# A hybrid decoder step on one core: where attention's merge, key casts, square roots and the sample's steps stand, and a second copy of v

## The chip, the cores and the metric

The kernel runs on one core of a Trainium2 chip. The core has five engines with instruction streams of their own: TensorE (PE in the profile; its weight loads are PEld), VectorE (DVE), ScalarE (ACT), GpSimd (POOL) and SyncE (SP), which here mostly issues transfers. Sixteen DMA engines carry the transfers. The metric is device time in microseconds (us) of one execution; the figure for a kernel is the median of its runs.

## The reference

One layer of a decoder is computed for a prompt of 2048 tokens and for a sample of 8 requests with 4 tokens each. All sizes: model width 1024, four recurrence heads of 128, eight attention heads of 64, hidden width 2816.

```python
a = rmsnorm(x, norm_attn_g)
qa, fa, ia, ga, qb, kb, vb = jnp.split(a @ w_in, pts, axis=-1)
s_new, o_a = gla_chunked(q_a, k_a, v_a, jnp.log(forget), hgrn_s0, chunk)
o_a = rmsnorm(o_a, hgrn_onorm_g) * jax.nn.silu(ga)
o_b = dilated_attn_prompt(q_b, k_b, v_b)      # the sample: against cached keys and values
h = x + jnp.concatenate([o_a, o_b], -1) @ w_o
...
h = h + (jax.nn.silu(c) * (hn @ w_up)) @ w_down
h = h + gate * (p_emb @ w_ple_proj)
```

The attention has three dilations, 1, 4 and 16, each over its own window. The parts of the dilations are combined by their maxima and sums (`combine_dilations`). The keys and values of the prompt, the recurrence's states and the sample's shifted caches are outputs too.

## The kernel before

**Stages.** `in_phase` runs twice, for 1024 and for 1056 tokens, and computes the seven projections. Each goes to a scratch tensor in DRAM: `qT_d` and `kT_d` with features on partitions, `v_d` by token, `ha_d` and `va_d` for the recurrence. During the first run, `down_weights` also prepares combinations of the down projection's weights, and in the second run most units of the recurrence (`hgrn_unit`) are computed. Then comes the attention stage (`attn_phase`), with the rest of the side work beside it, and then `trunk`: output projection (`out_block`), feed-forward block (`ffn_block`) and embedding block (`embed_block`), three blocks of tokens each.

**Attention by units and turns.** Four pairs of heads (p = 0 to 3) are worked off. Each has two passes (`di`): pass 0 takes queries and keys by residue modulo 4, pass 1 takes blocks of 128 neighbouring tokens. Both have four chunks (c) of 512 tokens. The masks hold the counts of the dilations, so that two passes serve for three. A pair has 40 units, so there are 160. The loop over x (here: a turn) gives each turn the scores of one unit (L814 and L815, with `kH` and `kL`, the rounded key and its remainder), then on VectorE the masked row minimum (L819) and on ScalarE the exponential (L820). Every second turn it transposes the probabilities of two older units (L827, copied out at L829) and multiplies those of two still older ones with v (L839). At pairs 0 to 2 all of pass 0 comes first; at pair 3 the passes alternate.

**What is hung on the turns.** A table `todo` holds functions by turn. `stage` loads q and k of the next chunk seven turns before `stack` splits them: `stack` rounds q on GpSimd (L152), takes the remainder (L704), casts k to `kH` on ScalarE (L707) and takes `kL` on GpSimd (L708). `values_chunk` loads v six turns before a chunk begins: in pass 0 by one transfer (L734), in pass 1 by four (L737), one for each residue, since the rows that go to one group of partitions are four tokens apart. When a chunk's pass 1 is summed, `merge` is hung on six later turns, +0, +2, +3, +7, +10 and +11: read the statistics of both passes back (L745), row minimum (L753) and weights, normalization (L757 to L760), transposition (L763) and the way of the coefficients through DRAM to all partitions (L766, L770, tile `cf`, two buffers), the products with the two partial outputs on GpSimd (L775), and their sum (L777), on VectorE for pairs 0 to 2 and on GpSimd for pair 3, which is stored to `mix_d`.

**Side work.** The generator `others` holds the recurrence's last unit (`hgrn_unit` with `apart=True`), the sample's attention (`attn_sample`) and the sample's recurrence (`hgrn_sample`). It advances by one step after each of the first 27 turns and then after every second turn, and what is left follows at the end. Its steps are traced with a higher priority.

**What sets the order.** In the attention stage PE's order is that of the program (`manual_schedule`). On all other engines, and on SP's queue, a planner decides from a simulated course of time when an instruction stands in its engine's stream; it may put an instruction ahead of others if it takes its inputs to be there. Each engine then works strictly in that order, so an instruction whose input is late holds all behind it. `keep_in_program_order` binds an instruction behind the one that the program issued before it on the same engine. `issue_after(recent[0].ins)` binds the loads for `down_weights` behind a named store on SP's queue.

**Roots.** The reciprocal root of a mean square is computed by `rsqrt_small` on VectorE: a shift and a subtraction on the integer form (L104, L105) and three rounds of three instructions (L107 to L109).

Of the kernel before, what the change touches and what calls it, by code (L numbers as in the profile page):

```python
# [16 lines left out]
ALU = mybir.AluOpType  # L17
# [31 lines left out]
def hymba_step_kernel(ctx: ExitStack, tc: tile.TileContext, I: dict, O: dict):  # L49
# [26 lines left out]
    ones = const.tile([128, 128], F32, name="ones")  # L76
    V.memset(ones, 1.0)

    mask = early.tile([128, 768], F32, name="mask")
    qT_s = early.tile([128, 4, NS], F32, name="qT_s")  # L80
    kT_s = early.tile([128, 4, NS], F32, name="kT_s")
# [3 lines left out]
    qT_d = dram.tile([128, 4, SEQ], F32, name="qT_d")  # L85
    kT_d = dram.tile([128, 4, SEQ], F32, name="kT_d")
    v_d = dram.tile([SEQ, 512], F32, name="v_d")
    va_d = dram.tile([SEQ, 512], F32, name="va_d")
    ha_d = [dram.tile([128, 4, NTOK], F32, name=f"ha{i}_d") for i in range(3)]
    mix_d = dram.tile([128, NK, NTOK], F32, name="mix_d")  # L90
# [5 lines left out]

    def f32(ap):
        return ap.bitcast(F32)

    def rsqrt_small(pool, v, shape):  # L100
        i = pool.tile(shape, I32, name="rs_i")
# [122 lines left out]
    def in_phase(bi, tiles, shared, wp, ev, sm, pmm, pms, plv, po):  # L224
# [102 lines left out]
        def token_group(g, kind, w):  # L327
            late = None

            for j in (0, 1, 8, 2, 3, 4, 5, 6, 7) if bi else range(8):  # L330
# [47 lines left out]
                if smp:  # L378
                    if kind in "kv":
                        for b in range(8):  # L380
                            SP.dma_start(O["s" + kind][b, SEQ - 4:SEQ], o[4 * b:4 * b + 4])
                else:
                    if kind == "k":
                        SP.dma_start(O["pk"][tok:tok + 128], o)
                    if kind == "v":
                        SP.dma_start(O["pv"][tok:tok + 128], o)
                        recent[:] = [SP.dma_start(v_d[tok:tok + 128], o)]
                    if kind == "i":
                        SP.dma_start(va_d[tok:tok + 128], o)
                yield  # L390
# [49 lines left out]
    def hgrn_unit(u, heads, S, ld, wk, sp, plv, po, pms, msk, diag, apart=False):  # L440
# [130 lines left out]
            yield  # L571
        v = sp.tile([128, 2, 4], F32, name="o_v")
        V.tensor_scalar(v, ssq, 1.0 / 128, EPS, op0=ALU.mult, op1=ALU.add)
        r = rsqrt_small(sp, v.rearrange("p h c -> p (h c)"), [128, 8])
        if apart:
            yield
        for i, h in enumerate(heads):
# [15 lines left out]
    def hgrn_sample(hp, pps):  # L593
# [76 lines left out]
        v = hp.tile([128, 1], F32, name="hsv")  # L670
        A.activation(o, ops, AF.Square, accum_out=v)
        V.tensor_scalar(v, v, 1.0 / 128, EPS, op0=ALU.mult, op1=ALU.add)
        r = rsqrt_small(hp, v, [128, 1])
        V.tensor_scalar(o, ops, r, None, op0=ALU.mult)
        yield
        pt = pps.tile([128, 4, 128], F32, name="s1")
# [8 lines left out]
    def attn_phase(spare, rest):  # L685
# [9 lines left out]
                out.append(t)  # L695
            return out

        def stack(c, q, k):
            cs = slice(512 * c, 512 * c + 512)
            js = slice(128 * c, 128 * c + 128)  # L700
            split = "p (i r) -> p r i"
            for hh in range(2):
                round_g(qS[:, hh, cs], q[:, hh])
                G.tensor_sub(qS[64:, hh, cs], q[64:, hh], f32(qS[64:, hh, cs]))  # L704
            for hh in range(2):
                t = k[:, hh].rearrange(split, r=4)
                A.copy(kH[:, hh, :, js], t)  # L707
                G.tensor_sub(kL[:, hh, :, js], t, f32(kH[:, hh, :, js]))  # L708

        first = stage(0, 0, [t[:, :1024].rearrange("p (h t) -> p h t", h=2) for t in spare])  # L710
# [18 lines left out]
        def values_chunk(p, di, c):  # L729

            raw = wk.tile([128, 4, 128], F32, name="v", bufs=6)
            cols = v_d[512 * c:512 * c + 512, 128 * p:128 * p + 128]
            if di == 0:
                SP.dma_start(raw, cols.rearrange("(i r) c -> i r c", r=4))  # L734
            else:
                for r in range(4):
                    SP.dma_start(raw[32 * r:32 * r + 32], cols.rearrange("(n i r) c -> r i n c", i=32, r=4)[r])  # L737
            vals[p, di, c] = raw

        stats_d = [dram.tile([SEQ, 4], F32, name=f"stat{p}_d") for p in range(4)]  # L740
        coef_d = [[dram.tile([16, 128], F32, name=f"coef{p}{c}_d") for c in range(4)] for p in range(4)]

        def merge(p, c, parts, both):

# [27 lines left out]
                             .to_broadcast([64, 1024]))  # L772
            yield
            for i in range(2):
                G.tensor_mul(parts[i], parts[i], cf[:, i])  # L775
            yield
            (G if p == 3 else V).tensor_add(parts[1], parts[1], parts[0])  # L777
            SP.dma_start(mix_d[:, 4 + p, 512 * c:512 * c + 512], parts[1])

        class Block:  # L780
# [82 lines left out]
        for p in range(4):  # L863
            for c in range(4):
                x = begin[p, 0, c]
                if p:

                    x = begin[p, 0, 0] - 10 + 4 * c
                    at(x - 7, lambda p=p, c=c: staged.append(stage(p, c)))
                    at(x, lambda p=p, c=c: stack(c, *staged.pop(0)))  # L870
                elif c:
                    at(x - 12, lambda c=c: staged.append(stage(0, c)))
                    at(x - 6, lambda c=c: stack(c, *staged.pop(0)))
                for di in range(2):
                    at(begin[p, di, c] - 6, lambda p=p, di=di, c=c: values_chunk(p, di, c))
# [4 lines left out]
        def sums(u, x):  # L880
# [5 lines left out]
            if bl.r == 3:  # L886
# [3 lines left out]
                if di == 0:  # L890
                    outs[c] = o
                    SP.dma_start(stats_d[p][512 * c:512 * c + 512].rearrange("(i r) c -> i r c", r=4),
                                 bl.st.rearrange("p n h c -> p n (h c)"))
                else:
                    merge_at([x + d for d in (0, 2, 3, 7, 10, 11)], p, c, (outs[c], o), bl.both)

        for x in range(n + 19):
            if x < n:
# [758 lines left out]
    with tc.manual_schedule(engines={mybir.EngineType.PE}):  # L1657
        for turn in itertools.count(1):
            if next(main) == "last":
                break  # L1660
            if turn % 2 == 0 or turn < 28:
                first(side, 1)
        first(side, 1000)
    step(main, 1000)
# [160 lines left out]
```

## Time and profile before

| | |
|---|---|
| median of 3 runs | 2998.84 us (2991.91 to 3001.22) |
| profiled execution | 2996.88 us |
| its span, first to last instruction | 2995.1 us |
| mean granted clock of TensorE | 0.987 |
| attention stage | about 825 to 1195 us of the span |
| trunk | from about 1193 us to the end |

The profile is one execution. Its groups, waits and windows give busy times and the idle time of an engine ahead of an instruction, with the engine or transfer that ended it ("<-"). A row of the order of time begins with its start and its length in us. TensorE's granted clock is a share of its full speed; at 0.5 a matmul takes twice as long.

### The profile page before, as it was taken

How to read it: one execution, taken by the hardware profiler on the slowest of the kernel's cores; microseconds unless marked ns; L12 is line 12 of the kernel's file. 1: busy time of each engine (PE TensorE's matmuls, PEld its weight loads, DVE VectorE, ACT ScalarE, POOL GpSimd, SP SyncE). 2: the span in 40 equal slices, each digit the busy share in tenths (PEclk: the TensorE clock that was granted, in tenths of full speed). 3: DMA queues.
4: the chain of work that ended last, by engine and by line, in shares of the span. 5: the costliest groups of instructions: out<-in, count | busy, mean ns of one | idle time of the engine just before them, and what ended most of it. 6: DMA issues, size and time to landing. Idle time of an engine off the chain costs nothing.

```text
span 2995.1 us, 52434 instructions
## 1 busy us (share of the span) xinstructions
PE 2899.1 (97%) x18895; PEld 2700.5 (90%) x18895; DVE 2163.4 (72%) x4717; ACT 1318.4 (44%) x2856; POOL 674.0 (23%) x792
## 2 busy tenths in 40 slices
PE   8999999999989898999999999999999999999998
PEld 8987789887777677999999999999999999999998
DVE  6656758657386467569987888766679777677777
ACT  5333423222276576335444444544444544444443
POOL 1443222212143563103443431000001000000000
PEclk9999999999999999999999999999999999999998
DMA  5898634324349996766766668777779777778773
GB/s 179 297 355 305 206 105 120 99 80 124 123 114 279 249 234 177 258 233 210 243 203 204 203 200 293 236 242 243 252 242 308 251 237 243 245 261 295 267 268 132
DMA packets 342036, 659.88 MB, mean 220 GB/s; under 512 B 62928, under 2 KB 134736, under 8 KB 339984
## 3 DMA queue, kind: packets, MB, share of 16 engines
q1 hardware_dynamic: 304928, 468.42, 49.0%
q0 software_dynamic: 33264, 121.13, 12.8%
q10 hardware_dynamic: 3584, 66.98, 6.2%
q8 instruction: 149, 2.44, 0.3%
q14 instruction: 111, 0.91, 0.1%
HBM read 509.46 MB, written 213.92 MB: 242 GB/s over the span
## 4 chain that ended last, share of the span: by engine, by line
PE 59%; issue 17%; DMA 10%; DVE 9%; POOL 2%; ACT 2%; SPq 1%; POOLq 0%; DVEq 0%; ACTq 0%
PE mm L146 13%; PE mm L148 13%; PE mm L147 13%; PE mm L348 2%; PE mm L349 2%; PE mm L350 2%; POOL w L1296 1%; DMA cf<-coef_d 1%; PE acc L839 1%; PE PT L827 1%; PE S L814 1%; DMA xr<-in_xT_dram 1%; PE lv L485 1%; DVE w L185 1%; DMA draw<-in_w_down_dram 1%
## 5 line engine op out<-in xcount | busy, mean ns | idle before, releaser
L147 PE MATMUL mm<-w 128*128 128x348 f32 (+3 forms) x3636 | 1166.1, 321 | 1.3 <-DVE w L1456 0.8
L146 PE MATMUL mm<-w 128*128 128x348 f32 (+3 forms) x3508 | 1108.7, 323 | 18.7 <-ACT s L1254 6.2
L148 PE MATMUL mm<-w 128*128 128x348 f32 (+3 forms) x3508 | 1117.3, 321 | 2.0 <-DVE w L185 2.0
L147 PEld LDWEIGHTS mm<-w 128*128 128x128 f32 x3636 | 684.1, 188 | 4.1 <-DVE w L1088 2.0
L146 PEld LDWEIGHTS mm<-w 128*128 128x128 f32 x3508 | 656.2, 188 | 26.6 <-ACT s L1254 8.7
L148 PEld LDWEIGHTS mm<-w 128*128 128x128 f32 x3508 | 659.0, 188 | 3.3 <-DVE w L185 2.6
L185 DVE TENSOR_TENSOR w<-raw,w 128x512 fp32r<-128x512 f32 x586 | 421.1, 723 | 176.2 <-ACT w L184 168.6
L184 ACT CAST w<-raw 128x512 fp32r<-128x512 f32 x586 | 360.9, 621 | 413.1 <-PE mm L148 288.8
L1296 POOL DMA_DIRECT2D w<-wd_d x231 | 124.3, 538 | 899.2 <-PE mm L148 793.4
L1312 DVE TENSOR_TENSOR h<-h,mm 128x348 f32<-128x348 f32 (+1 forms) x504 | 247.7, 507 | 44.8 <-PE mm L148 43.5
L820 ACT ACTIVATE P<-P,st 128x256 f32<-128x256 f32 (+3 forms) x256 | 134.0, 526 | 60.0 <-DVE st L819 56.4
L1254 ACT COPY s<-mm 128x348 f32<-128x348 f32 (+1 forms) x198 | 88.0, 445 | 152.2 <-PE mm L148 151.9
L819 DVE CUSTOM_DVE_ANT_0 P<-S,mask 128x256 f32<-128x256 f32 (+3 forms) x256 | 104.4, 448 | 62.0 <-PE S L815 40.2
L348 PE MATMUL mm<-wh,xh 128*128 128x512 f32 x352 | 140.8, 403 | 0.1
L349 PE MATMUL mm<-wl,xh 128*128 128x512 f32 x352 | 140.7, 401 | 0.2 <-DVE wl L271 0.2
L350 PE MATMUL mm<-wh,xl 128*128 128x512 f32 x352 | 140.3, 399 | 0.0
L146 PE MATMUL mm<-xh,wh 128*128 128x384 f32 (+2 forms) x384 | 124.6, 329 | 8.0 <-ACT xh L246 5.2
L148 PE MATMUL mm<-xh,wl 128*128 128x384 f32 (+2 forms) x384 | 124.4, 328 | 4.2 <-DVE wl L271 4.2
L147 PE MATMUL mm<-xl,wh 128*128 128x384 f32 (+2 forms) x384 | 125.0, 328 | 1.2 <-DVE xl L247 1.2
L185 DVE TENSOR_TENSOR dw<-draw,dw 128x512 fp32r<-128x512 f32 x77 | 75.3, 981 | 54.0 <-ACT dw L184 53.6
L152 POOL TENSOR_SCALAR wh<-wraw 128x512 fp32r<-128x512 f32 x96 | 75.3, 798 | 133.3 <-PE mm L147 41.6
L814 PE MATMUL S<-kH,qS 128*128 128x256 f32 (+3 forms) x256 | 98.6, 400 | 6.7 <-DVE st L819 4.2
(346 smaller groups left out, 5053.2 us busy)
## 6 DMA issues: line engine op xcount, KB each, us to landing
w<-wd_d POOLq DMA_DIRECT2D x231, 512.0 KB, 5.5
wd_d<-dw SPq DMA_DIRECT2D x77, 512.0 KB
out_sk_dram<-in_cache_k_dram ACTq DMA_DIRECT2D x56, 584.0 KB
out_sv_dram<-in_cache_v_dram ACTq DMA_DIRECT2D x56, 584.0 KB
raw<-in_w_gate_dram SPq DMA_DIRECT2D x110, 256.0 KB
raw<-in_w_up_dram SPq DMA_DIRECT2D x110, 256.0 KB
wraw<-in_w_in_dram SPq DMA_DIRECT2D x104, 256.0 KB
raw<-w_gate_d SPq DMA_DIRECT2D x88, 256.0 KB
```

What stands on the lines that cost most here:

```text
L146: PE.matmul(ps, lhsT=wh, rhs=xh, start=first, stop=False, skip_group_check=read)
L147: PE.matmul(ps, lhsT=wh, rhs=xl, start=False, stop=False, skip_group_check=read)
L148: PE.matmul(ps, lhsT=wl, rhs=xh, start=False, stop=last, skip_group_check=read)
L184: A.copy(w[:, 0], raw)
L185: V.tensor_sub(w[:, 1], raw, f32(w[:, 0]))
L348: PE.matmul(ps, lhsT=xh[k][:, js], rhs=wh, start=k == 0, stop=False)
L349: PE.matmul(ps, lhsT=xh[k][:, js], rhs=wl, start=False, stop=False)
L350: PE.matmul(ps, lhsT=xl[k][:, js], rhs=wh, start=False, stop=k == NK - 1)
L814: PE.matmul(s[:, w * i:w * i + w], lhsT=bl.q(hh), rhs=bl.k(kH, hh), start=True, stop=False)
L820: A.activation(pe, pe, AF.Exp, bias=mn, scale=-1.0, accum_out=st[:, bl.r, hh, 0:1])
L1296: G.dma_start(t, wd_d[p][n - 1])
L1312: V.tensor_add(o, o, acc[m][:, :H])
```

## The change

1. `rsqrt_pow` computes a root as one power instruction on GpSimd, with a constant column of -0.5. The recurrence's unit with `apart=True` and the sample's recurrence use it; all other roots stay.
2. `v_r` is a second copy of v in DRAM. Each 128 tokens are stored in it ordered by residue modulo 4, by a second store of the same tile. Pass 1 of the attention reads a chunk from it by one transfer in place of four. `recent` names this second store.
3. In `stack`, the casts of k for pairs 1 to 3 keep their place in the program's order on ScalarE.
4. In `merge`, the two products and the sum keep their place on GpSimd and on VectorE (GpSimd for pair 3). For pairs 0 to 2 the products are hung on turn +14 in place of +10, and the sum on +16 in place of +11.
5. The side work advances after the turns that leave 0, 2 or 4 modulo 7, and after turn 136 also after those that leave 1 or 5, where it was every second turn. The first 27 turns stay as they were.

```diff
+    root = const.tile([128, 1], F32, name="root")
+    G.memset(root, -0.5)
...
+    v_r = dram.tile([SEQ, 512], F32, name="v_r")
...
+    def rsqrt_pow(pool, v, shape):
+        y = pool.tile(shape, F32, name="rs_y")
+        G.tensor_tensor(y, v, root.to_broadcast(shape), op=ALU.pow)
+        return y
...
-                        recent[:] = [SP.dma_start(v_d[tok:tok + 128], o)]
+                        SP.dma_start(v_d[tok:tok + 128], o)
+                        recent[:] = [SP.dma_start(v_r[tok:tok + 128].rearrange("(r i) c -> i r c", r=4), o)]
...
-        r = rsqrt_small(sp, v.rearrange("p h c -> p (h c)"), [128, 8])
+        r = (rsqrt_pow if apart else rsqrt_small)(sp, v.rearrange("p h c -> p (h c)"), [128, 8])
...
-        r = rsqrt_small(hp, v, [128, 1])
+        r = rsqrt_pow(hp, v, [128, 1])
...
-        def stack(c, q, k):
+        def stack(c, q, k, late=lambda ins: ins):
...
-                A.copy(kH[:, hh, :, js], t)
+                late(A.copy(kH[:, hh, :, js], t))
...
-            cols = v_d[512 * c:512 * c + 512, 128 * p:128 * p + 128]
-            if di == 0:
-                SP.dma_start(raw, cols.rearrange("(i r) c -> i r c", r=4))
-            else:
-                for r in range(4):
-                    SP.dma_start(raw[32 * r:32 * r + 32], cols.rearrange("(n i r) c -> r i n c", i=32, r=4)[r])
+            cols = (v_d, v_r)[di][512 * c:512 * c + 512, 128 * p:128 * p + 128]
+            SP.dma_start(raw, cols.rearrange(("(i r) c -> i r c", "(r i) c -> i r c")[di], r=4))
...
+        late = tc.keep_in_program_order
...
-                G.tensor_mul(parts[i], parts[i], cf[:, i])
-            yield
-            (G if p == 3 else V).tensor_add(parts[1], parts[1], parts[0])
+                late(G.tensor_mul(parts[i], parts[i], cf[:, i]))
+            yield
+            late((G if p == 3 else V).tensor_add(parts[1], parts[1], parts[0]))
...
-                    at(x, lambda p=p, c=c: stack(c, *staged.pop(0)))
+                    at(x, lambda p=p, c=c: stack(c, *staged.pop(0), tc.keep_in_program_order))
...
-                    merge_at([x + d for d in (0, 2, 3, 7, 10, 11)], p, c, (outs[c], o), bl.both)
+                    merge_at([x + d for d in ((0, 2, 3, 7, 14, 16) if p < 3 else (0, 2, 3, 7, 10, 11))], p, c, (outs[c], o), bl.both)
...
-            if turn % 2 == 0 or turn < 28:
+            if turn < 28 or turn % 7 in (0, 2, 4) or (turn > 136 and turn % 7 in (1, 5)):
```

## The prediction

> **What bounds the kernel now.** I read the page's first part, then the busy time by windows, then TensorE's waits, and last the order of time around the longest waits.
>
> ```profile
> span 2995.1 us, 52434 instructions
> PE 2899.1 (97%) x18895; PEld 2700.5 (90%) x18895; DVE 2163.4 (72%) x4717; ACT 1318.4 (44%) x2856; POOL 674.0 (23%) x792
> ```
>
> TensorE (PE) is busy nearly throughout, and no matmul is added or removed. So the change can only take away, or add, time in which PE waits or runs at a lowered clock. It touches the attention stage, from 825 to 1195 us, and a little of the projections before. Windows (length; busy PE, PEld, DVE, ACT, POOL; granted clock; DMA share; GB/s):
>
> ```profile
> 100.00:350.00 250.00, 242.98 (x1200) 204.26 (x1199) 168.02 (x295) 86.16 (x154) 96.53 (x89) 0.99 0.86 308
> 825.00:1195.00 370.00, 334.82 (x2956) 261.71 (x2955) 245.43 (x868) 243.66 (x708) 170.06 (x203) 0.94 0.81 209
> 900.00:1110.00 210.00, 194.96 (x1697) 143.10 (x1697) 122.56 (x446) 137.66 (x404) 106.21 (x127) 0.95 0.99 258
> 895.00:905.00 10.00, 5.81 (x35) 5.31 (x36) 8.93 (x27) 5.31 (x19) 6.53 (x10) 0.66 0.70 203
> 1009.00:1021.00 12.00, 7.54 (x39) 4.47 (x39) 1.77 (x10) 6.93 (x22) 7.18 (x8) 0.57 1.11 240
> 1100.00:1113.00 13.00, 11.56 (x67) 9.48 (x66) 3.81 (x23) 8.33 (x31) 10.00 (x15) 0.61 0.70 181
> ```
>
> In the attention stage PE idles 370 - 334.8 = 35 us, and the clock is at 0.94. The last three rows are spots where a wait is followed by a lowered clock. The clock's loss there is 10 x 0.34 = 3.4, 12 x 0.43 = 5.2 and 13 x 0.39 = 5.1 us; I count only the share in which PE was busy (0.58, 0.63, 0.89): 2.0, 3.3 and 4.5 us. What PE waited for in this stage (total, times, longest):
>
> ```profile
> PE PT L827 <- ACT P L820: 6.0, 5, 4.0
> PE s L586 <- DVE at L579: 4.8, 1, 4.8
> PE S L814 <- DVE st L819: 4.2, 5, 1.8
> PE mm L146 <- ACT w L1087: 3.4, 1, 3.4
> PE s L946 <- DMA skt<-in_kT_d_dram: 1.6, 2, 1.2
> PE s L986 <- DMA skt<-in_v_d_dram: 1.6, 2, 1.2
> PE s L677 <- DVE hso L674: 1.4, 1, 1.4
> PE s L986 <- DMA skt<-in_v_w_dram: 0.8, 1, 0.8
> ```
>
> **The root of the recurrence's last unit.** The order of time around the 4.8 us wait:
>
> ```profile
> 890.80 2.55 POOL L704 TENSOR_TENSOR qS<-stage,qS 64x512 fp32r<-64x512 f32 x2
> 892.40 0.98 DVE L104 TENSOR_SCALAR rs_i<-o_v 128x8 int32<-128x8 int32 x1
> 893.73 3.01 POOL L708 TENSOR_TENSOR kL<-stage,kH 128x512 fp32r<-128x512 f32 x2
> 895.81 0.95 DVE L107 TENSOR_TENSOR rs_t<-rs_y 128x8 f32<-128x8 f32 x1
> 898.24 0.17 DVE L109 SCALAR_TENSOR_TENSOR rs_y<-rs_t,rs_y 128x8 f32<-128x8 f32 x1
> 898.44 1.29 DVE L579 TENSOR_TENSOR at<-at,rs_y 128x512 f32<-128x512 f32 x2
> 899.19 1.11 PE L586 MATMUL s<-c_ident,at 128*128 128x128 f32 x4 [4.80 <-DVE at L579]
> ...
> L758 POOL TENSOR_TENSOR mn<-wl 128x8 f32<-128x8 f32 x16 | 3.8, 236 | 1.1
> L708 POOL TENSOR_TENSOR kL<-stage,kH 128x512 fp32r<-128x512 f32 x30 | 46.3, 1559 | 17.4 <-PE s L946 9.5 <-ACT kH L707 7.4
> ```
>
> The eleven small DVE instructions take from 892.40 to 898.41, because attention's work stands between them and two shown here take nearly 1 us each while POOL's work runs, against 0.17 later. One power instruction on POOL replaces them. No row shows its price; it lies between the 0.24 us of a POOL product of the same 128x8 shape and the 1.56 us of one of 128x512. I take 0.5: near the first by shape, doubled since a power is more work. The other question is its place. Right behind L704, which ends at 893.35, it is done at 893.9 and half of L579 at 894.6, while PE waits since 899.19 - 4.80 = 894.39: a wait of 0.2, so 4.6 us are saved, and the 2.0 of the clock. Behind both L708, at 896.74, the wait is still 3.5: 1.3 saved. The first is nearer, since L708 must also wait for a cast that the change puts later. I take **-5** (bounds -6.6 and 0).
>
> **The key casts in program order.** At two spots ScalarE (ACT) took up a key cast L707 whose load had not landed, and the exponentials L820 stood behind it:
>
> ```profile
> 1010.71 2.12 ACT L707 CAST kH<-stage 128x512 fp32r<-128x512 f32 x2 [5.89 <-DMA stage<-kT_d]
> 1012.26 0.18 DVE L753 TENSOR_REDUCE mn<-st 128x8 f32<-128x16 f32 x1 [5.55 <-DMA st<-stat_d]
> 1013.38 1.17 PE L827 MATMUL PT<-c_ident,P 128*128 128x128 f32 x4 [4.04 <-ACT P L820]
> ...
> 1099.40 2.14 ACT L707 CAST kH<-stage 128x512 fp32r<-128x512 f32 x2 [2.67 <-DMA stage<-kT_d]
> 1102.10 1.18 PE L827 MATMUL PT<-c_ident,P 128*128 128x128 f32 x4 [1.00 <-ACT P L820]
> ```
>
> The loads are issued seven turns ahead of the cast's place in the program. The stage's 370 us hold 167 turns, 2.2 us each, so a cast that keeps its place comes 15 us after its load's issue and need not wait 5.9. Its result is wanted ten turns after that. At the first spot DVE too was held, until 1012.26, by the merge's minimum L753, which the change leaves free to move; so I count half: 2.0 of 4.04, and half of 3.3 for the clock. At the second, the whole 1.0 and half of 4.5 for the clock. That is -2.0 - 1.65 - 1.0 - 2.25 = **-6.9** (bounds 0, and all of it: 4.0 + 3.3 + 1.0 + 4.5 = -12.8). Casts now stand behind the exponentials of their turn; what then is late is POOL's L708, for which ten turns are left.
>
> The Trainium skill, "TensorE: Matmul & The Clock Gate", Part 1, has the clock halved only after an idle window of about 3.4 us. The second spot, 1.00 us of wait with a clock of 0.61, doesn't fit it, the first does. By that rule the first spot would give its whole clock loss and the second none, -2.0 - 3.3 - 1.0 = -6.3 in place of -6.9.
>
> **The end of merge.** VectorE (DVE) takes up the sum L777 before POOL's products L775, which wait for coefficients on their way:
>
> ```profile
> L775 POOL TENSOR_TENSOR o<-o,cf 128x512 f32<-128x512 f32 x32 | 42.5, 1350 | 99.8 <-DMA cf<-coef_d 98.4 <-ACT w L184 1.4
> L777 DVE TENSOR_TENSOR o<-o,o 128x512 f32<-128x512 f32 x12 | 10.2, 846 | 20.7 <-POOL o L775 20.7
> ```
>
> Fixed in order and four turns (9 us) later, both should find their data. But 20.7 us of idle DVE reached PE only as part of its 4.2 us behind L819, which has other causes too; I take half: **-2.1** (bounds -4.2 and, by a queue that it may block, a loss: the slower rival).
>
> **The sample's pace.** It has 92 steps, counted in the code: 27 in the first turns, then every second turn, so the last is at turn 156. With three and then five of seven it is at turn 161. Loads for the sample's attention spread over 14% more turns while the DMA share is 0.99; of 4.0 us of waits on skt I take half, **-2** (bounds -4.0, 0). After that its work is dense beside the last head pair, and its end is five turns, 11 us, later. SP's queue at that place:
>
> ```profile
> 1179.74 0.46 SPq L679 DMA_DIRECT2D mix_d<-hsg  x1
> 1180.25 4.07 SPq L1011 DMA_DIRECT2D raw<-in_w_o_dram  x3
> ...
> 1192.80 0.59 PE L146 MATMUL mm<-w 128*128 128x348 f32 x2 [3.44 <-ACT w L1087]
> ```
>
> The trunk's first weight loads stand right behind the sample's last write. If they must follow it, the trunk starts up to 11 us later; but nothing in the program ties them, so I take **+1.5** (bounds 0 and 11). The sample's root, in the same way on POOL, gives **-1** of its 1.4 (bounds -1.4, 0).
>
> **v a second time.** SP's issues (count: shortest/median/longest ns):
>
> ```profile
> L737 SPq DMA_DIRECT2D v<-v_d x64: 303/428/2286, 835.6 to 1170.0; - x64
> L387 SPq DMA_DIRECT2D v_d<-ev x16: 422/574/1128, 181.7 to 827.3; - x16
> ...
> 827.25 0.43 SPq L387 DMA_DIRECT2D v_d<-ev  x1
> 827.78 1.25 SPq L693 DMA_DIRECT2D stage<-kT_d  x2
> ...
> PE mm L148 <- DVE wl L271: 3.6, 2, 3.0
> ```
>
> Sixteen writes of 256 KB are added, 4.2 MB, or 13.6 us of traffic at the 308 GB/s of the first window, half of it while that window's DMA share is 0.86. Weights arrive there on the same queue, and the last row, from PE's waits between 100 and 400 us, is PE waiting for their split. I take **+1.5** (bounds 0, 6.8). One more issue ahead of attention's first key load: **+0.6**. Sixteen loads stand for 64: 48 x 0.43 = 20.6 us less of SP's issuing, behind which other loads stood; no row of PE's waits above names v, so I take nothing. That is covered by loads made six turns ahead.
>
> **The sum**: -5 - 6.9 - 2.1 - 2 + 1.5 - 1 + 1.5 + 0.6 = **-13.4 us**. The profiled execution took 2996.88 us around its span of 2995.1, and lies 2 us below the median of 2998.84. From the median: 2985.4, so **2985 us**, 0.46% faster. Its own range, terms at half and at most of their bounds: 2974 to 2991.
>
> **Rivals.** *The waits only move.* Between 900 and 1110 us the DMA share is 0.99, and the loads for casts, merges and sample all share it; PE then waits for a stage or skt load where it waited for ACT. For it: L753, which isn't fixed, held DVE at the very spot that the cast held ACT. Against it: the DMA waits that PE itself shows are 4.0 us. Only the two roots (-6) remain, less 3.6 for v and the late end: about **2996**, no change.
>
> *The late merge blocks SP.* The coefficients have two buffers; a merge takes one at turn +7 and now frees it at +14 instead of +10, and merges start four turns apart, so the third asks at +15, one turn after. If POOL, now in program order behind a chunk's casts, is more than that turn (2.2 us) late, SP's in-order queue stands, and key, v and skt loads with it. One stop costs what the 1013 us spot did, 4.0 + 3.3 = 7.3; three of them, one for each of the first head pairs, give +22, against the -13.4 without its merge term, -11.3: +10.7, about **3010**, slower; it decides from two such stops on. For it: POOL idled 98.4 us on these coefficients, and the casts' subtractions of one chunk take it 2.55 + 3.01 = 5.6 us. Against it: the loads are issued six and seven turns ahead, and POOL is busy under half the stage.
>
> *The change doesn't do what it says*: the power stands behind L708 and the casts find late loads all the same; then -1.3 - 2.1 - 2 + 3.6 = -1.8, no change, counted with the first rival.
>
> **Chances.** Forecast 0.55, waits that move 0.28, blocked queue 0.17. About 0.3%, 9 us, is what a measurement of this kernel can tell from no change, its three runs spreading over 9.3 us. The forecast's low edge loses a little below that bound and the first rival's high edge gains a little: faster 0.55, same 0.28, slower 0.17. The range reaches from savings twice my sum, 2970 or so, well into the slower rival, to 3006.
>
> **What would show it.** Root: L586 waits under 1 us, the clock near 1 after it. Casts: ACT's idle time before L707 on stage loads, 5.89 and 2.67 us at the two spots, falls to near nothing, and no stretch after 1005 us at half clock. Merge: L777 behind L775 under 5 us. v: 32 loads in place of 80. Wrong: a cf issue that SP waits for by several us, a longer wait at the trunk's first matmul, a power of several us, or new half-clock stretches elsewhere in the stage.

## The result and the profile after

The changed kernel takes **3009.3 us** in the median of six runs (3006.01 to 3013.03), the kernel before 2997.52 beside it. The ratio is 1.0040, with a 95% interval of 1.0029 to 1.0051: slower by 0.4%, where 0.46% faster was forecast. The profiled execution took 3006.01 us, at a granted clock of 0.985 (before: 0.987).

The experiments below end somewhere else than the trace of this kernel alone would lead: **most or all of the loss comes from the constant of -0.5**, which takes 32 bytes in each partition and moves nearly every tile behind it. So the profile after is read twice, first for what each part did to its own spot, and later for the whole.

The first part of the page, and windows as in the prediction (length; busy PE, PEld, DVE, ACT, POOL; granted clock; DMA share; GB/s), after. All fences below show chosen rows; rows between them are left out:

```profile
span 3004.2 us, 52374 instructions
PE 2907.9 (97%) x18895; PEld 2707.8 (90%) x18895; DVE 2166.0 (72%) x4695; ACT 1319.7 (44%) x2856; POOL 670.7 (22%) x795
```

```profile
825.00:1195.00 370.00, 336.58 (x2945) 263.69 (x2943) 241.54 (x840) 240.07 (x699) 170.92 (x205) 0.94 0.82 206
895.00:905.00 10.00, 4.84 (x44) 4.30 (x44) 9.31 (x20) 5.57 (x13) 9.08 (x11) 0.92 1.08 289
1009.00:1021.00 12.00, 9.67 (x68) 7.75 (x68) 5.69 (x27) 7.74 (x26) 10.48 (x15) 0.86 1.08 243
1036.00:1047.00 11.00, 6.68 (x34) 4.04 (x35) 3.18 (x8) 2.23 (x7) 2.77 (x3) 0.53 1.06 239
1100.00:1113.00 13.00, 13.00 (x121) 9.22 (x120) 5.41 (x29) 10.20 (x35) 4.89 (x6) 1.00 0.80 172
```

At the three spots that the prediction meant to mend, the clock rose from 0.66, 0.57 and 0.61 to 0.92, 0.86 and 1.00. But there is a new stretch at 0.53, the fourth row, which the prediction named as a sign of being wrong. The stage as a whole shows the same mean clock, 0.94, and from the first score to the first matmul of the trunk it takes 371.5 us instead of 364.9. TensorE's waits in 825 to 1225 us (total, times, longest) show what came instead:

```profile
PE PT L770 <- DVE pt L836: 6.6, 2, 6.4
PE PT L834 <- DVE pt L836: 6.0, 2, 4.8
PE S L821 <- DVE st L826: 5.2, 4, 2.3
PE mm L154 <- ACT w L1094: 3.7, 1, 3.7
PE s L624 <- POOL hsF L615: 3.1, 1, 3.1
PE s L595 <- DVE at L588: 1.7, 1, 1.7
PE PT L834 <- ACT P L827: 1.4, 3, 0.9
PE s L686 <- DVE hso L683: 0.6, 1, 0.6
```

The waits on loads `skt` (the sample's cached keys and values) are gone, that for the exponentials (L827, before L820) fell from 6.0 to 1.4 us, that of the root (L595, before L586) from 4.8 to 1.7. The first two rows, 12.6 us of waiting for VectorE's copies `pt` of the transposed probabilities, were 1.8 us before. New are 3.1 us on GpSimd's `hsF`, a factor of the sample's recurrence.

**The root.** The order of time, after:

```profile
891.06 2.53 POOL L713 TENSOR_TENSOR qS<-stage,qS 64x512 fp32r<-64x512 f32 x2
893.85 1.68 POOL L105 TENSOR_TENSOR rs_y<-o_v,root 128x8 f32<-128x8 f32 x1
895.57 1.33 DVE L588 TENSOR_TENSOR at<-at,rs_y 128x512 f32<-128x512 f32 x2 [1.18 <-POOL rs_y L105]
896.34 0.66 PE L595 MATMUL s<-c_ident,at 128*128 128x128 f32 x4 [1.69 <-DVE at L588]
...
899.02 6.11 DVE L940 COPY qb<-qT_s 64x32 f32<-64x32 f32 x8
899.10 2.54 POOL L713 TENSOR_TENSOR qS<-stage,qS 64x512 fp32r<-64x512 f32 x2
901.72 2.99 POOL L717 TENSOR_TENSOR kL<-stage,kH 128x512 fp32r<-128x512 f32 x2
906.00 1.94 PE L834 MATMUL PT<-c_ident,P 128*128 128x128 f32 x8 [4.81 <-DVE pt L836]
```

The power stands where it was expected, behind the remainder of q, and takes 1.68 us. Ten microseconds later VectorE copies q for the sample (`qb`) while GpSimd does the remainders of q and k; the eight copies take 6.11 us, and TensorE waits 4.81 for the copy behind them. The profile of before has these copies too:

```profile
902.74 3.52 DVE L933 COPY qb<-qT_s 64x32 f32<-64x32 f32 x8
902.96 2.51 POOL L704 TENSOR_TENSOR qS<-stage,qS 64x512 fp32r<-64x512 f32 x2
```

There they took 3.52 us, 2.51 of them beside GpSimd's remainder of q; the remainder of k, which waited for its cast, began at 906.75, behind them. After, 5.5 of the 6.11 us lie beside remainders. That this is the cause shows in the single copies. In all twenty traces, the 64 copies that begin while a remainder runs end 0.03 to 0.04 us behind its end, after 0.3 to 1.5 us; the 81 that find GpSimd idle take 0.17 to 0.18 us each. Before, TensorE waited only 0.83 us here. From the first to the 65th score, which lies behind both spots, it is 93.1 us before (93.6 when that kernel was profiled again) and 94.1 after: what was gained at the root is gone.

**The merge.** Groups, and the order of time at a spot that is new:

```profile
L782 POOL TENSOR_TENSOR o<-o,cf 128x512 f32<-128x512 f32 x32 | 41.7, 1327 | 92.6 <-DMA cf<-coef_d 92.6
L784 DVE TENSOR_TENSOR o<-o,o 128x512 f32<-128x512 f32 x12 | 10.3, 861 | 14.5 <-POOL o L782 14.5
L716 ACT CAST kH<-stage 128x512 fp32r<-128x512 f32 x30 | 32.6, 1138 | 3.0 <-DMA stage<-kT_d 3.0
```

```profile
1024.17 4.70 SPq L777 DMA_DIRECT2D cf<-coef_d  x2
...
1036.50 2.48 POOL L782 TENSOR_TENSOR o<-o,cf 128x512 f32<-128x512 f32 x2 [15.36 <-DMA cf<-coef_d]
...
1039.02 0.69 DVE L784 TENSOR_TENSOR o<-o,o 128x512 f32<-128x512 f32 x1 [6.80 <-POOL o L782]
1039.63 1.01 DVE L836 COPY pt<-PT 128x384 f32<-128x384 f32 x2
...
1040.32 0.37 PE L770 MATMUL PT<-c_ident,w 128*16 128x128 f32 x1 [6.42 <-DVE pt L836]
```

ScalarE's idle time ahead of the key casts fell to 3.0 us from the 14.6 of this row of before:

```profile
L707 ACT CAST kH<-stage 128x512 fp32r<-128x512 f32 x30 | 32.7, 1141 | 14.6 <-DMA stage<-kT_d 11.1 <-PE S L814 2.6 <-PE S L815 0.9
```

But VectorE still stands idle for 14.5 us ahead of the sums, where it was 20.7: the coefficients, issued at 1024, are what is late, and a sum that now has to keep its place holds the copy `pt` behind it for 6.80 us, and through it TensorE. The place is only part of it: with the merge as before (u_merge, below), the longest wait of this kind is still 3.3 us.

### The profile page after: what moved, and what is told of

The parts are those of the page before. It is cut to its first block, busy times and chain, and to the rows that moved or that the text cites. A ratio compares the mean times of both kernels' runs of the same rounds, so it can differ in the third digit from the quotient of the medians.

```text
span 3004.2 us, 52374 instructions
## 1 busy us (share of the span) xinstructions
PE 2907.9 (97%) x18895; PEld 2707.8 (90%) x18895; DVE 2166.0 (72%) x4695; ACT 1319.7 (44%) x2856; POOL 670.7 (22%) x795
## 3 DMA queue, kind: packets, MB, share of 16 engines
q1 hardware_dynamic: 306464, 472.61, 49.5%
## 4 chain that ended last, share of the span: by engine, by line
PE 74%; DMA 9%; DVE 9%; issue 3%; POOL 2%; ACT 2%; SPq 1%; DVEq 0%; POOLq 0%; ACTq 0%
PE mm L154 18%; PE mm L156 18%; PE mm L155 18%; PE mm L356 2%; PE mm L358 2%; PE mm L357 2%; DMA cf<-coef_d 1%; PE acc L846 1%; DMA stage<-qT_d 1%; DMA wd_d<-dw 1%; PE PT L834 1%; PE S L821 1%; DVE h L1319 1%; DMA draw<-in_w_down_dram 1%; PE lv L494 1%
## 5 line engine op out<-in xcount | busy, mean ns | idle before, releaser
L827 ACT ACTIVATE P<-P,st 128x256 f32<-128x256 f32 (+3 forms) x256 | 134.3, 527 | 72.1 <-DVE st L826 71.0
L279 DVE TENSOR_TENSOR wl<-wraw,wh 128x512 fp32r<-128x512 f32 x104 | 88.1, 869 | 33.5 <-POOL wh L160 28.5
```

The costliest lines, as they stand in the source:

```text
L827: A.activation(pe, pe, AF.Exp, bias=mn, scale=-1.0, accum_out=st[:, bl.r, hh, 0:1])
```

## The experiments

All ratios are to the kernel before in the same session, with 95% intervals.

### Each part undone

Four kernels, each the changed one with one part as it was before (u_pace, u_merge, u_root, u_vr), and a fifth with the key casts free again (u_kh):

```diff
u_pace
-            if turn < 28 or turn % 7 in (0, 2, 4) or (turn > 136 and turn % 7 in (1, 5)):
+            if turn % 2 == 0 or turn < 28:
u_merge
-                late(G.tensor_mul(parts[i], parts[i], cf[:, i]))
+                G.tensor_mul(parts[i], parts[i], cf[:, i])
-            late((G if p == 3 else V).tensor_add(parts[1], parts[1], parts[0]))
+            (G if p == 3 else V).tensor_add(parts[1], parts[1], parts[0])
-   ((0, 2, 3, 7, 14, 16) if p < 3 else (0, 2, 3, 7, 10, 11))
+   (0, 2, 3, 7, 10, 11)
u_root
-        r = (rsqrt_pow if apart else rsqrt_small)(sp, ...)
+        r = rsqrt_small(sp, ...)
-        r = rsqrt_pow(hp, v, [128, 1])
+        r = rsqrt_small(hp, v, [128, 1])
u_vr
-            cols = (v_d, v_r)[di][512 * c:512 * c + 512, 128 * p:128 * p + 128]
+            cols = v_d[512 * c:512 * c + 512, 128 * p:128 * p + 128]   # four loads in pass 1, no store of v_r
u_kh
-                    at(x, lambda p=p, c=c: stack(c, *staged.pop(0), tc.keep_in_program_order))
+                    at(x, lambda p=p, c=c: stack(c, *staged.pop(0)))
```

> The changed kernel with the sample's steps after every second turn again; all else as changed. The changed kernel took 3009.3 us, the one before 2997.5. Theory 'late, dense end': TensorE was 3.4 us ahead of before at score 22 of 24 and 4.9 behind at the last, so undoing the pace gives back about 8 us: 3001. Theory 'the pinned sum': the loss comes from VectorE standing 6.8 us before the merge's sum, which stays: 3007 to 3010, and a wait of 5 us or more on VectorE's copies remains in the profile. Theory 'chance in the trunk': the 5.6 us that the changed kernel lost between 1421 and 1504 us, where the instructions stand in the same order as before, come and go with the clock's phase whatever is undone.

> The changed kernel with merge as before: products and sum not bound to the program's order, at turns +10 and +11; all else as changed. Theory 'the pinned sum': the wait of 6.4 us at 1040 us and the lowered clock behind it (about 3 us) go, 9 us: 3000. Theory 'late, dense end': no more than 2 us of difference, 3007 to 3010, since the end of the stage has pair 3, whose turns are the same.

> The changed kernel with both roots on VectorE again. The power on GpSimd took 1.68 us, and the wait before the last unit's transposes 1.69 in place of 4.80 before. Theory of the prediction, root term: undoing it costs 3 to 5 us: 3013. Rival: what the root saved was lost 10 us later, at 906 us, where TensorE waited 4.81 us for VectorE (the score at 909 us comes 0.6 us later than before, not earlier): no difference, 3009, and the wait at 906 us is gone.

> The changed kernel with v kept once and the four loads per chunk of pass 1 again. Prediction: the second store cost 2 us and gave nothing, 3007. Rival: fewer issues on SP's queue helped by up to 5 us, so undoing it makes the kernel slower, 3012 to 3015.

> The changed kernel with the casts of keys free to move again; all else as changed. So far, against the kernel before: changed 1.0040, pace undone 1.0018, merge undone 1.0041, roots undone 1.0059, v's copy undone 1.0050. No part undone alone takes the loss away but half of it with the pace. Theory 'casts': the casts in order make ScalarE late for the exponentials at turns where it was early before, and undoing them gives 1.001 to 1.002. Theory of the prediction: they save 7 us, so undoing them gives 1.006.

Measured: 1.0018 (1.0004 to 1.0031) without the pace, 1.0041 (1.0025 to 1.0058) without the merge's, 1.0059 (1.0037 to 1.0081) without the roots, 1.0050 (1.0033 to 1.0068) without the second v, 1.0041 (1.0029 to 1.0053) without the casts. Only the pace, undone, makes a difference to the 1.0040 of the whole; and with it undone the waits on the sample's loads are back, in u_pace's waits:

```profile
PE s L953 <- DMA skt<-in_kT_d_dram: 3.5, 1, 3.5
PE s L993 <- DMA skt<-in_v_d_dram: 3.5, 2, 3.2
PE s L993 <- DMA skt<-in_v_w_dram: 1.6, 1, 1.6
```

So the pace does remove these waits, and costs more than they did. But no single part explains the loss.

### Each part alone

The kernel before with the pace alone (o_pace), with the roots alone (o_root), with the casts alone (o_kh), with roots, casts and second v together (u_pm), and the kernel before once more under another name (again). The edits are the ones shown above, the other way round.

> The kernel before with the new pace of the sample's steps alone (v's copy, merge, casts and roots as before; the constants of the change stay, unused). Theory 'pace': the late, dense end alone costs 6 us or more, 1.002 to 1.004, and the last 16 scores take 30 us in place of 21. Theory 'only together': alone it is no slower than before, 0.999 to 1.001, and the loss needs the bound merge.

> The kernel before with the roots on GpSimd, the casts in order and v's copy; pace and merge as before. If pace and merge hold the whole loss and the other three the gains that I forecast (roots 5, casts 7, v's copy 2 lost): 0.997, faster. If the loss is of the casts or of v's copy: 1.002 or more. If the parts only shift waits: 0.999 to 1.001.

> The kernel before once more, for a second profile of it. All kernels with a part undone show, as the changed one does, 3 to 6 us more than before between 1414 and 1464 us of the span, where VectorE is busy throughout, the instructions stand in the same order, and a wait of 2.5 us is followed by half the clock. If that is chance of the clock's phase, this profile of the kernel before shows it too, or the like at another place; if it is the change's doing (an address, a transfer left over), it shows 49.5 us there again. The time is 1.000 within 0.1%.

> Before, with the two roots on GpSimd alone. Theory A (gain given back: the wait ahead of the transposes of the recurrence's last unit falls from 4.8 to under 2 us, and a wait of 4 to 5 us for DVE's copy of the transposed weights appears 10 us later, behind the sample's copies of q): stage within 3 us of before, ratio 0.998 to 1.002. Theory B (the roots are what makes roots, casts and second v together slower by 0.24%): ratio 1.002 to 1.004. My recorded prediction had -6 us, ratio 0.998.

> Before, with only the key casts fixed in program order. Recorded prediction: -6.9 us, ratio 0.998. Theory A (the stalls of 4.0 and 1.0 us ahead of the transposes at 1013 and 1102 us go, and others of the same sum take their place): ratio 0.999 to 1.001. Theory B (the casts are what makes roots, casts and second v together slower by 0.24%, since an exponential then waits for a cast that waits for its load): ratio 1.002 to 1.004.

Measured: pace alone 1.0060 (1.0047 to 1.0073), roots alone 1.0048 (1.0029 to 1.0066), casts alone 1.0059 (1.0042 to 1.0075); roots, casts and second v together 1.0024 (1.0013 to 1.0036); the kernel before against itself 1.0001 (0.9990 to 1.0012). Each part alone thus loses more than all of them together. A theory in which each part has a price of its own can't give that. With the roots alone, the wait at their place (L594) is 3.0 us instead of 4.8; with the casts alone, ScalarE stands 6.3 us before them instead of 14.6. Both do what they were made for, and both kernels are half a per cent slower.

The casts alone do more than that. In their trace the root is still on VectorE, and yet the wait at L594 is 3.15 us, the copies `qb` meet both remainders, and TensorE waits for the copy behind them:

```profile
896.58 1.11 PE L594 MATMUL s<-c_ident,at 128*128 128x128 f32 x4 [3.15 <-DVE at L587]
900.13 6.04 DVE L943 COPY qb<-qT_s 64x32 f32<-64x32 f32 x8
902.94 3.01 POOL L716 TENSOR_TENSOR kL<-stage,kH 128x512 fp32r<-128x512 f32 x2
907.05 1.23 PE L837 MATMUL PT<-c_ident,P 128*128 128x128 f32 x8 [2.99 <-DVE pt L839]
```

With the roots alone the copies meet the remainders too, in two pieces (2.38 and 2.85 us), and a wait of 2.50 us on VectorE follows. So either part alone shortens the root's wait, and either alone brings the collision behind it.

Two kernels with other paces, again on the kernel before, were to part the late end from the dense steps:

```diff
p_120
+            if turn < 28 or turn % 7 in (0, 2, 4) or (turn > 120 and turn % 7 in (1, 5)):
p_dense
+            if turn < 28 or (turn % 2 == 0 if turn <= 136 else turn % 7 in (0, 1, 2, 4, 5)):
```

> Before, with the sample's steps at three of seven turns and, from turn 120 instead of 136, at five of seven: its last step is then at the same turn as in the kernel before, five turns earlier than with the change's pace. Theory A (the late end costs: the sample ends beside or behind the last scores, and the trunk waits for it): no change from before, 2990 to 3000 us, ratio 0.998 to 1.001, and the stage from the first score to the first trunk matmul at 362 to 366 us. Theory B (a thin middle followed by dense steps costs, whenever it ends): slower as with the pace alone, ratio 1.004 to 1.007, stage near 375 us.

> Before, with every second turn kept until turn 136 and five of seven after it, so that only the dense part is added and the sample ends some six turns earlier than before. Theory A (the late end costs): no loss, ratio 0.997 to 1.001. Theory B (dense steps beside the last head pair cost, by waits for their loads and by a lowered clock): slower by about half of the pace's loss or more, ratio 1.003 to 1.006. A third theory, that the thin middle alone costs, expects no loss here, and a loss in the run beside this one.

Measured: 1.0071 (1.0055 to 1.0087) and 1.0063 (1.0041 to 1.0084). A sample that ends no later than before, or earlier, loses as much: the late end isn't the cause. By then, eleven kernels that differ from the kernel before in quite different lines were all slower, by 0.2 to 0.7%. What they have in common is that the constant `root` and the tensor `v_r` are set up in all of them, used or not.

### The place of the tiles

The constant has four bytes in each partition and takes 32. In the programs' lists of addresses, 4066 of 4664 tiles in the engines' memory stand 32 bytes further when it is there; where `v_r` isn't used, it moves no other tensor in DRAM (in o_pace and u_vr, two small ones of the merge changed places). So the constant was tried by itself, set and read by nothing, at three sizes. The order of instructions on every engine is that of the kernel before, but for the one that sets it.

```diff
+    root = const.tile([128, 1], F32, name="root")     # pad32; 16 columns in pad64, 64 in pad256
+    G.memset(root, -0.5)
```

The whole change was run with the constant widened in the same way (after64, after256), and with the constant made where a root is taken, in a tile that is freed behind it (after0), which leaves all but some two dozen of 4662 tiles where the kernel before has them:

```diff
after0
-    root = const.tile([128, 1], F32, name="root")
-    G.memset(root, -0.5)
...
+        root = pool.tile(shape, F32, name="rs_t")
+        G.memset(root, -0.5)
         y = pool.tile(shape, F32, name="rs_y")
-        G.tensor_tensor(y, v, root.to_broadcast(shape), op=ALU.pow)
+        G.tensor_tensor(y, v, root, op=ALU.pow)
```

> Before, with nothing of the change but the 128x1 constant of the roots: it is set and used by nothing, and moves nearly every tile of the chip's memory behind it up by 32 bytes; the order of every engine's instructions is the same. Theory L (the place of the tiles, common to all the runs so far that were not the kernel before itself, costs about half a per cent): ratio 1.004 to 1.006. Theory T (the kernel before is timed so closely that any new order in the attention stage loses 5 to 15 us): ratio 0.999 to 1.001.

> The same with a constant of 128x16, so that the tiles move by 64 bytes. Theory L, if a boundary of 64 bytes is what matters: ratio 0.999 to 1.001; if a larger boundary or the place itself matters: 1.003 to 1.006. Theory T: 0.999 to 1.001.

> The whole change, with the constant of the roots made 128x16, so that the tiles lie 64 bytes and not 32 behind those of the kernel before. Theory L: the loss goes, ratio to before 0.995 to 1.000. Theory T: as the change, ratio 1.003 to 1.005.

> The whole change, with that constant made 128x64: the tiles lie 256 bytes behind those of before. Theory L with any boundary up to 256 bytes: ratio 0.995 to 1.000, also where the run with 64 bytes doesn't gain. Theory T: 1.003 to 1.005.

> The whole change, with the constant of the roots made where a root is taken, in a tile that is freed behind it: all tiles but nine stand where the kernel before has them. Theory L (the 32 bytes are what costs): ratio 0.997 to 1.000, since the change with the tiles moved by 256 bytes was at 1.0014. Theory T (new orders lose): 1.002 to 1.005. My recorded prediction, made without thinking of the place of tiles: 0.9954.

> Before, with an unused constant of 128x64: every tile 256 bytes further, order unchanged. It is what the change moved by 256 bytes (ratio 1.0014) is to be compared with. Theory L with a boundary above 64 bytes: 0.999 to 1.001, and then the change itself costs 0.1%. If any other place costs as 64 bytes did (1.0018): 1.001 to 1.003, and then the change itself costs nothing.

| tiles moved by | kernel before | with the whole change |
|---|---|---|
| 0 | 1.0001 (0.9990 to 1.0012) | 1.0014 (0.9998 to 1.0029) |
| 256 bytes | 1.0004 (0.9990 to 1.0018) | 1.0014 (1.0000 to 1.0029) |
| 64 bytes | 1.0018 (1.0006 to 1.0031) | 1.0035 (1.0021 to 1.0050) |
| 32 bytes | **1.0041** (1.0026 to 1.0056) | **1.0040** (1.0029 to 1.0051) |

An unused constant alone, with nothing of the change, gives the whole measured loss; the five runs of pad32 lie at 3001.86 to 3007.33 us. pad64 and pad256 set their constant by the same instruction, so it is the place of the tiles that costs and not the setting. Taken out of the change (after0 for the changed kernel), the 32 bytes give back 0.26%, to within 0.19. Across the rows, the change in the right column stands 0.13, 0.10, 0.17 and -0.01% above the left one. The mean is +0.10%, and with the intervals taken as independent it is known to about 0.10%: a loss of some 3 us, between 0 and 6, and no gain.

So the main point of theory L holds: pad32 lies in its range and far from that of theory T. Its ranges for the whole change don't. They expected a gain, below 1.000, once the tiles stood well, and after0 and after256 came out at 1.0014, after64 at 1.0035; pad64 fell between its two cases. Theory T missed pad32, pad64, after0 and after256.

Read anew against pad32, which ran in another session, the single parts are: pace +0.19%, roots +0.07, casts +0.18, roots, casts and second v together -0.17, each to within about 0.2%. Only two comparisons leave that noise, and both are the pace: undone in the whole change it gives back 0.22% (1.0040 against 1.0018, to within 0.17), and with the dense part from turn 120 it is 0.30% above pad32 (to within 0.22). A kernel with roots, casts and second v, no pace and no moved tile may thus be the best of all; it was not run, and its gain would be near the limit of what can be measured.

**Where the 32 bytes cost time.** The order of time of pad32 (its L830 is L827 before, L949 is L946, L989 is L986):

```profile
900.49 1.12 PE L589 MATMUL s<-c_ident,at 128*128 128x128 f32 x4 [4.74 <-DVE at L582]
...
937.12 0.85 PE L949 MATMUL s<-skt,qb 128*32 128x384 f32 x8 [1.59 <-DMA skt<-in_kT_d_dram]
...
987.55 1.93 PE L989 MATMUL s<-skt,sPT 96*32 96x512 f32 x8 [2.84 <-DMA skt<-in_v_d_dram]
...
1019.10 1.18 PE L830 MATMUL PT<-c_ident,P 128*128 128x128 f32 x4 [5.19 <-ACT P L823]
...
1111.09 1.18 PE L830 MATMUL PT<-c_ident,P 128*128 128x128 f32 x4 [2.75 <-ACT P L823]
```

The first row is the root's wait, as long as before (4.80). Three of the others are longer than before, and each follows a load: the sample's load of 2.84 us, where the longest such wait was 1.2 us before and 1.6 in a second execution of that kernel (the 1.59 us above is no more than that), and the two spots where a cast waits for a key load, 5.19 and 2.75 instead of 4.04 and 1.00. The sample's waits alone don't single pad32 out: in pad64, whose stage is no longer than before, the longest is 2.9 us, and in pad256 2.4. Of the waits for the exponentials, the row of pad64 is

```profile
PE PT L830 <- ACT P L823: 4.6, 2, 4.3
```

and that of pad32

```profile
PE PT L830 <- ACT P L823: 8.6, 4, 5.2
```

All these waits lie in or next to the stretch in which the DMA engines are full. Windows over it, of before, pad32 and pad64 in turn (the last three columns are granted clock, DMA share, GB/s):

```profile
930.00:1080.00 150.00, 137.56 (x1217) 98.97 (x1209) 85.20 (x293) 91.32 (x260) 65.65 (x72) 0.97 1.03 266
```

```profile
930.00:1080.00 150.00, 134.41 (x1181) 98.09 (x1177) 79.48 (x274) 86.31 (x246) 59.91 (x68) 0.94 1.02 257
```

```profile
930.00:1080.00 150.00, 133.86 (x1188) 97.87 (x1191) 83.01 (x288) 88.62 (x256) 62.95 (x71) 0.95 1.04 266
```

At the same full share pad32 moves 257 GB/s, against 266 in the kernel before and with 64 bytes. That alone doesn't show that transfers take longer, since a kernel that runs later for another reason also asks for less. The times of the single packets in the traces say more. Between 825 and 1195 us, in single executions (the DMA time is the packets' time, divided by 16 engines):

| tiles moved by | kernels | DMA time per MB moved | mean of a 512-byte packet |
|---|---|---|---|
| 0 or 256 bytes | before, again, pad256, after0, after256 | 3.75 to 3.85 us | 32.5 to 33.3 ns |
| 64 bytes | pad64, after64 | 3.92 to 3.94 us | 34.6 to 35.6 ns |
| 32 bytes | the other thirteen kernels | 3.92 to 4.08 us | 35.1 to 37.2 ns |

So in this stage transfers do take longer, by some 5% in the mean, in every kernel whose tiles are moved by 32 or 64 bytes. Ahead of the stage the same packets take 27.1 to 27.6 ns in all of them. The Trainium skill, "DMA: Bandwidth & Descriptors", "How a descriptor splits into AXI transactions", has a descriptor cost extra beats when it doesn't start on a boundary of 256 bytes. The tiles `stage`, `v` and `cf` start on such a boundary before; by that rule 64 bytes would slow them as well as 32, and the packets agree with that, though the rate of 266 GB/s in the one window doesn't show it. Whether 64 bytes cost less time than 32 is hardly settled: alone they are 0.23% apart, to within 0.20, and with the whole change 0.05. How the slower transfers become 0.4%, and why pad64's stage is no longer than before, stays open.

The stage's parts in single executions, in us (from the starts of the first and the 241st of the 256 score matmuls of `kH`, and of the trunk's first matmul):

| kernel | 1st to 241st score | 241st score to trunk | both |
|---|---|---|---|
| before | 333.6 | 31.3 | 364.9 |
| again | 330.8 | 30.9 | 361.7 |
| pad256 | 333.9 | 31.8 | 365.7 |
| pad64 | 334.6 | 30.7 | 365.4 |
| pad32 | 339.9 | 32.7 | 372.6 |
| after0 | 323.6 | 39.4 | 362.9 |
| after256 | 325.4 | 39.0 | 364.4 |
| after64 | 327.2 | 40.7 | 367.9 |
| after (32) | 329.5 | 41.9 | 371.5 |

Down each half of the table 32 bytes cost 7 to 11 us of the stage against no move or 256 bytes. Across, at equal place of the tiles, the change is 7 to 10 us ahead at the 241st score and gives back 7 to 10 in the last turns. Most of both is the sample's work, moved: TensorE's time for it behind the 241st score is 3.4 us before and 11.0 in after0.

TensorE's waits in after0, the change with no tile moved, over its stage:

```profile
PE PT L834 <- DVE pt L836: 5.7, 3, 4.8
PE s L624 <- POOL hsF L615: 4.3, 1, 4.3
PE mm L154 <- ACT w L1094: 4.1, 1, 4.1
PE S L821 <- DVE st L826: 4.1, 2, 2.2
PE PT L770 <- DVE pt L836: 2.1, 2, 1.9
PE s L595 <- DVE at L588: 1.7, 1, 1.7
```

These waits belong to the change, then, and not to the 32 bytes: `pt` behind the copies `qb`, 4.8 us, and `hsF`, 4.3. The 6.42 us at the merge's pinned sum are 1.9 here, and GpSimd's products begin 11.0 us behind the issue of their coefficients, where it was 12.3.

## Why the prediction was wrong

**The step that failed is one that isn't there.** The prediction weighed nearly every instruction that the change adds, moves or removes, and had no term for the constant itself: it names the power that reads the column, and the column nowhere. Its place in memory cost 0.41% (pad32), about 12 us, more than any term of the sum; taken out of the whole change it gives back 0.26%, about 8 us. The sum of -13.4 us for the rest was wrong as well: by the four pairs of kernels it is about +3, between 0 and +6. The second rival's number, 3010 us, lies within 1 us of the measured 3009.3; that is luck, since its mechanism was another.

**Root, -5: the mechanism held, the gain didn't.** The place behind the remainder of q was right; the power took 1.68 us, not 0.5, and the wait fell by 3.1 us (4.80 to 1.69), not 4.6. About half of that fall is the casts': alone they bring it to 3.15, the roots alone to 2.98. What is late next was the step left out: the copies `qb` met both of GpSimd's remainders, where before the remainder of k came behind them, and TensorE waited 4.81 us ten microseconds later. Roots or casts alone bring this on too, with 2.50 and 2.99 us. From the first to the 65th score nothing is gained, at no moved tile either (94.1 us in after0, 93.1 before).

**Key casts, -6.9: the stalls went, the time went elsewhere.** ScalarE's idle time ahead of the casts fell from 14.6 to 3.0 us and the two spots run at clocks of 0.86 and 1.00, nearly as forecast; that no stretch after 1005 us would be at half clock was wrong (0.53 from 1036 to 1047 us). Alone on the kernel before they are within noise of pad32. The first rival, that waits only move, had this right and, as forecast for it, held for the contents of the change as a whole.

**Merge's end, -2.1.** L784 was to stand under 5 us behind L782 and stands 14.5: not the planner's order was late but the coefficients. The second rival looked for the blocked queue on SP. SP did stand longer ahead of these issues, 31 us in all and at most 7.4, against 14 and 2.6 before. But only 2.1 us of it were for GpSimd's products, the wait that the rival named, and with the merge undone the sum is nearly the same, 30. What the change's own merge blocked was VectorE, held 6.80 us by the sum that must keep its place. In time no difference can be seen: 1.0041 without it, 1.0040 with it.

**Pace, -2 and +1.5.** The waits on `skt` went, as forecast. That its dense steps only move work into the last turns, 7.6 us of it, was counted through the trunk's first weights alone, at +1.5; TensorE's wait for those went from 3.4 to 3.7 us. By the two comparisons that leave the noise, the pace costs 0.2 to 0.3%; why that is more than the single executions show stays open.

**Sample's root, -1.** The wait L686 fell from 1.4 to 0.6 us. **v, +1.5 and +0.6.** The first score begins at 827.2 us, 827.9 before: the sixteen added stores cost nothing that can be seen, and with the second v undone the ratio was 1.0050 against 1.0040.

**The trunk** was not to change and has a spot that did: 290 of its matmuls, from the 1381st on, take 55.0 to 55.1 us in all four kernels with the whole change and in pad32, and 49.5 to 53.7 in before, again, pad64 and pad256. It looks like the change's doing, which isn't shown: the two executions of the kernel before differ by 2.8 us there, and p_120, o_pace and o_root, whose tiles are moved by 32 bytes too, take 49.5, 50.8 and 51.0. What goes with the time is the clock, which in the clock's record is halved here for 0 us (49.5 and 50.8), 3.4 (51.0 to 52.4), 6.8 (53.7) or 10.2 (55.0 to 55.2). There is a wait, and then a lowered clock, with the same instructions in the same order. The wait and a window behind it, after:

```profile
1431.31 0.43 PE L154 MATMUL mm<-w 128*128 128x348 f32 x1 [2.52 <-ACT s L1261]
```

```profile
1430.00:1440.00 10.00, 8.15 (x32) 7.71 (x33) 6.79 (x19) 4.76 (x12) 1.27 (x1) 0.66 0.50 158
```

The rule of the Trainium skill that the prediction weighed ("TensorE: Matmul & The Clock Gate", Part 1), a halved clock only after some 3.4 us of idling, doesn't agree with this wait of 2.52 us either.

## What to carry to other kernels

Before the price of a change is looked for in its instructions, run the kernel before with only the change's new tiles, unused: here a constant of four bytes a partition cost 0.4%, as much as the verdict on five edits. When every part, undone or alone, gives the same sign and the parts don't add up, look for what all the kernels share. And where a wait is shortened on a path that several engines pace, ask which instruction now meets which work on another engine: here what was gained at the root was lost ten microseconds later. A spot that differs between two single executions may be chance, as in the trunk; a second execution of the same kernel tells.

## What was not expected of the hardware

- Moving the tiles by 32 bytes costs 0.41% (0.26 to 0.56), by 64 bytes 0.18% (0.06 to 0.31), by 256 bytes nothing (0.04%, -0.10 to 0.18). In the attention stage the DMA engines then need 3.92 to 4.08 us per MB, against 3.75 to 3.85 with no move or 256 bytes.
- A power on GpSimd takes 1.68 us for 128x8, seven times the 0.24 us of a product of that shape.
- Eight copies of 64x32 on VectorE take 6.11 us with 5.5 us of GpSimd's remainders beside them, and 3.52 us with 2.5 us of them. A copy that begins while a remainder runs ends 0.03 to 0.04 us behind it; one with GpSimd idle takes 0.17 to 0.18 us.
